# A decoder layer's 32 experts: blocks of 72 to 124 slots in float32r products in place of 64 + 32 and 128

## The chip, the core and the metric

The kernel runs on one core of one Trainium2 chip. A time is the device time of one execution, in microseconds (us); a verdict comes from the medians of repeated runs of both kernels on the same chip. Before the change three runs took 2187.02, 2189.25 and 2190.99 us, median 2189.25 us. All rows below come from one further execution, recorded by the hardware profiler, which took 2188.17 us.

Names used throughout: PE is TensorE (matmuls; PEld is its weight loading), DVE is VectorE, ACT is ScalarE, POOL is GpSimd, SP is SyncE, which issues the large loads.

## What is computed

One layer of a decoder: sliding-window attention and a convolution branch, a layer norm, then a mixture of experts and a second layer norm. Only the mixture of experts matters here. 1024 tokens of width 1024 are each sent to 4 of 32 experts, so 4096 places are shared out unevenly.

```python
logits = h @ w_router + b_router
top_val, top_idx = lax.top_k(logits, TOP_K)          # TOP_K = 4 of 32
gates = softmax(top_val)
# for each expert e, over its tokens xb:
act = clamped_swiglu(xb @ w_up[e] + b_up[e])         # 1024 -> 2048 -> 1024
ys  = act @ w_down[e] + b_down[e]                    # 1024 -> 1024
y_moe[token] += gate * ys
```

An expert has 12 MB of float32 weights (w_up 1024 x 2048, w_down 1024 x 1024). All of it is read from HBM once, whatever the number of its tokens.

## The kernel before, in words

The first 640 us (attention, convolution, output projection, router) are not touched. The mixture of experts follows, from about 640 to 2130 us, then the second layer norm to the end at 2186.6 us.

**Slots.** The router ranks the experts by the number of their tokens. The program is written for ranks, not for experts: rank j has a fixed number of slots, `CAPS[j]`, from 320 for the fullest to 64 for the emptiest, and reads at run time which expert holds the rank. Tokens beyond the slots would be done in a loop behind the main part, one block of 128 at a time; with these inputs it runs zero times. The names p0 to p31 in the profile are ranks.

**Blocks.** The slots of a rank are cut into blocks that PE works on. Before the change a block is 128, 64 or 32 slots wide. A block of 128 (called *wide* here) holds its tokens as the stationary operand, 128 columns, and streams 512 columns of weights at a time. If the rank is *split*, every weight tile and every activation is written as a high and a low part in float32r (`split`, L85 to L87: ACT copies the high part, DVE subtracts it to get the low part), and a product is three float32r matmuls: high x high, high x low, low x high (L251). A block of 64 or 32 uses the unsplit float32 weights: the columns of the PE array are divided into 2 or 4 groups, each of which works on another piece of the output columns at the same time (L260). A rank is split if it has a wide block (`self.split`); it keeps its raw weights until the matmuls are done if it also has a narrow block (`self.keep`).

**Steps.** Each expert is 12 steps of 256 rows of weights (1 MB): steps 0 to 3 and 4 to 7 make the two halves of the up projection, 8 to 11 the down projection. Ranks are worked on in pairs, `PAIRS`, so that a full and an empty one share the time in which weights arrive. Within a pair the order is: first rank's steps 0 to 3, second rank's 0 to 3, first's 4 to 7, second's 4 to 7, first's 8 to 11, second's 8 to 11: 24 steps a pair, 16 pairs.

**What sets the order.** The engines' queues are in program order, and the program is written step by step:

```python
for g, (e, s) in enumerate(G):
    split_ahead(g)      # weights split up to AHEAD = 6 half-steps ahead: this step and two more
    e.mm(s, ...)        # the matmuls of the step
    if g == 200: overflow()
    load_ahead(g)       # SP: as many 512 KB weight tiles as the 24 slots W0..W23 let it
    behind(g)           # what is due after this step, sorted by kind
```

`behind` places, among other things, for each expert: the transposes of its tokens (`x_T`, L165) shortly before its first step; after steps 3 and 7 the activation (`swiglu`, L270 to L276: bias add, sigmoid, two clamps, product; on DVE but for the sigmoid); after the step that follows, and after step 8, the transposes of the activation (`act_T`, L296), which are then split or copied; after step 11 the scaling by the gate on ACT and the scattered addition into the output in HBM on POOL's DMA queue (`scatter`, L319). So in DVE's queue an activation stands behind the splits of two later steps and ahead of all others. The program also computes, at step g = 200, which blocks the loop behind would need (`overflow`, L1227 to L1256, mostly DVE); g = 200 is the ninth step of the ninth pair.

**Biases.** For a wide block a row of 512 biases is loaded on POOL's queue (`load_row`, L210) and spread over the partitions by POOL (`bias_of`, L225). For a narrow block the DMA itself spreads it, in 2 or 4 pieces (`load_bias`, L220).

**Memory.** The 24 slots of 512 KB hold raw weights, high parts and low parts alike: a split step takes 2 raw tiles and 4 more once it is split, an unsplit one only 2.

## Time and profile before

| what | value |
|---|---|
| median of three runs | 2189.25 us |
| profiled execution | 2188.17 us |
| its span, first to last instruction | 2186.6 us |
| PE busy | 2069.1 us, 95% of the span |
| DVE busy | 1377.5 us, 63% |
| ACT busy | 878.9 us, 40% |
| POOL busy | 496.8 us, 23% |
| moved by the 16 DMA engines | 506.92 MB, 232 GB/s on the mean |

Busy shares are means over stages that differ. A matmul's recorded time reaches from its start to its modelled end, and matmuls overlap: the price of one is the distance from its start to the next one's start, not its recorded time. How the pairs of experts compare is read from the windows table among the rows below, whose stretches begin with the first matmul of a pair and end with the first of the next.

### The profile page before, as it was taken

To read this page: it belongs to the slowest core of one execution; us is meant where nothing else is said; L and a number is where in the kernel's file an instruction comes from. 1 tells how busy PE (TensorE), PEld (TensorE's weight loads), DVE (VectorE), ACT (ScalarE), POOL (GpSimd) and SP (SyncE) were. 2 spreads that over 40 slices of the span, in tenths; PEclk is the share of its full clock that TensorE was granted. 3 is DMA by queue.
4 is the path that set the end of the run, shared out by engine and by line. 5 is a ranking of instruction groups with operands and counts; after the bars stand their busy time and mean duration, and the time that the engine had idled before them with its cause. 6 is when DMAs were issued, how large, how long until landed. Compare 5 with 4: busy or idle time off the path is not lost. (4 is left out here: it accounts for less than half of the span.)

```text
span 2186.6 us, 31962 instructions
## 1 busy us (share of the span) xinstructions
PE 2069.1 (95%) x10925; PEld 1370.3 (63%) x10925; DVE 1377.5 (63%) x2052; ACT 878.9 (40%) x1337; POOL 496.8 (23%) x643
## 2 busy tenths in 40 slices
PE   8999999999959999999999999989999999999990
PEld 7776788887635566576654355556676466766760
DVE  3768799665845564656964126365596569569635
ACT  3155511432323433435653123334455357356521
POOL 1000000003332222323241322122243241232204
PEclk9999999999979999999999999999999999999995
DMA  5111112142339988998998997899889898988944
GB/s 161 41 37 30 30 49 58 34 139 64 107 116 326 313 289 301 362 347 266 319 312 296 345 333 259 283 335 328 281 312 285 307 305 303 357 259 314 346 161 162
DMA packets 191096, 506.92 MB, mean 232 GB/s; under 512 B 34700, under 2 KB 70974, under 8 KB 190929
## 3 DMA queue, kind: packets, MB, share of 16 engines
q1 hardware_dynamic: 163062, 448.86, 57.9%
q0 software_dynamic: 26592, 52.21, 9.9%
q10 hardware_dynamic: 1275, 3.77, 0.4%
q8 instruction: 87, 1.43, 0.3%
q14 instruction: 80, 0.66, 0.1%
HBM read 471.26 MB, written 33.49 MB: 231 GB/s over the span
## 5 line engine op out<-in xcount | busy, mean ns | idle before, releaser
L600 DVE SCALAR_TENSOR_TENSOR c<-a,cw,c 128x1024 f32<-128x1024 f32 x120 | 154.0, 1284 | 3.3
L828 POOL DMA_DIRECT2D bu<-in_b_up_dram x2 | 1.0, 502 | 456.4 <-DVE wol L87 456.4
L139 POOL DMA_DIRECT2D slt<-tab x103 | 54.5, 530 | 26.3 <-issue 12.5
L90 PE MATMUL ga<-xh,whga 128*128 128x512 f32 x128 | 52.1, 407 | 0.0
L92 PE MATMUL ga<-xh,wlga 128*128 128x512 f32 x128 | 50.5, 395 | 0.0
L91 PE MATMUL ga<-xl,whga 128*128 128x512 f32 x128 | 50.5, 394 | 0.0
L92 PE MATMUL gb<-xh,wlgb 128*128 128x512 f32 x128 | 50.4, 394 | 0.0
L90 PE MATMUL gb<-xh,whgb 128*128 128x512 f32 x128 | 50.4, 394 | 0.0
L91 PE MATMUL gb<-xl,whgb 128*128 128x512 f32 x128 | 50.4, 394 | 0.0
L1021 POOL DMA_INDIRECT tab<-rec,dst x32 | 32.7, 1021 | 59.5 <-DMA tab<-rec,dst 58.3
L927 PE MATMUL wo<-woh,mh 128*128 128x512 f32 x128 | 37.1, 424 | 0.6 <-ACT mh L86 0.6
L87 DVE TENSOR_TENSOR p8l<-p8w,p8h 128x1024 fp32r<-128x1024 f32 x24 | 29.5, 1281 | 10.3 <-ACT p8h L86 6.3
L927 PE MATMUL wo<-woh,ml 128*128 128x512 f32 x128 | 35.9, 404 | 0.0
L87 DVE TENSOR_TENSOR p7l<-p7w,p7h 128x1024 fp32r<-128x1024 f32 x24 | 29.3, 1270 | 9.8 <-ACT p7h L86 9.7
L927 PE MATMUL wo<-wol,mh 128*128 128x512 f32 x128 | 35.0, 409 | 0.0
L441 ACT ACTIVATE gt<-ga,pcol 128x512 f32<-128x512 f32 x16 | 11.0, 690 | 59.2 <-PE ga L92 59.1
L643 DVE SCALAR_TENSOR_TENSOR sc<-s,mask 128x512 f32<-128x512 f32 (+1 forms) x32 | 19.5, 652 | 23.9 <-PE s L640 21.8
L87 DVE TENSOR_TENSOR p0l<-p0w,p0h 128x1024 fp32r<-128x1024 f32 x24 | 29.6, 1270 | 7.4 <-ACT p0h L86 7.1
L87 DVE TENSOR_TENSOR p11l<-p11w,p11h 128x1024 fp32r<-128x1024 f32 x24 | 29.8, 1295 | 4.8 <-ACT p11h L86 4.6
L87 DVE TENSOR_TENSOR p1l<-p1w,p1h 128x1024 fp32r<-128x1024 f32 x24 | 28.5, 1241 | 5.0 <-ACT p1h L86 4.8
L87 DVE TENSOR_TENSOR p15l<-p15w,p15h 128x1024 fp32r<-128x1024 f32 x24 | 27.9, 1219 | 5.6 <-issue 4.7
L87 DVE TENSOR_TENSOR p13l<-p13w,p13h 128x1024 fp32r<-128x1024 f32 x24 | 27.9, 1219 | 5.4 <-ACT p13h L86 5.2
(1240 smaller groups left out, 6381.8 us busy)
## 6 DMA issues: line engine op xcount, KB each, us to landing
p6w<-in_w_up_dram SPq DMA_DIRECT2D x16, 512.0 KB
p31w<-in_w_up_dram SPq DMA_DIRECT2D x16, 512.0 KB
p1w<-in_w_up_dram SPq DMA_DIRECT2D x16, 512.0 KB
p30w<-in_w_up_dram SPq DMA_DIRECT2D x16, 512.0 KB
p13w<-in_w_up_dram SPq DMA_DIRECT2D x16, 512.0 KB
p19w<-in_w_up_dram SPq DMA_DIRECT2D x16, 512.0 KB
p2w<-in_w_up_dram SPq DMA_DIRECT2D x16, 512.0 KB
p29w<-in_w_up_dram SPq DMA_DIRECT2D x16, 512.0 KB
```

Source lines behind the costliest of these rows:

```text
L87: nc.vector.tensor_tensor(lo, src, hi.bitcast(F32), op=ALU.subtract)
L90: nc.tensor.matmul(o, ah, bh, start=start, stop=False)
L91: nc.tensor.matmul(o, ah, bl, start=False, stop=False)
L92: nc.tensor.matmul(o, al, bh, start=False, stop=stop)
L139: nc.gpsimd.dma_start(self.m[g * w:(g + 1) * w, i, :], tab[bass.ds(row + c, w), :])
L441: nc.scalar.activation(GT[c][:, sl], t, AF.Sigmoid, bias=bin_c(14 + c))
L600: nc.vector.scalar_tensor_tensor(C[c], A[c][:, w:w + S], cw[:, c, w:w + 1], C[c], op0=ALU.mult, op1=ALU.add)
L643: nc.vector.scalar_tensor_tensor(SC[b][c0 // 2][:, g::2, :W], t[g][:, :, :W], 0.125, mk[:, None, :].to_broadcast([P, 2, W]), op0=ALU.mult, ...
L828: nc.gpsimd.dma_start(bu, b_up[:, i * S:(i + 1) * S])
L927: nc.tensor.matmul(t, ml[:, k, :], W[k][:, sl], start=n == 0, stop=n == 3 * KC - 1)
L1021: nc.gpsimd.indirect_dma_start(out=tab[:, :], out_offset=bass.IndirectOffsetOnAxis(ap=DST[b][:, k:k + 1], axis=0), in_=REC[:, b, k, :], in ...
```

## The change

`CAPS` becomes the sum of a new table, `WIDTHS`, that gives each rank its blocks. A block is packed into column groups only if it is 64 or 32 wide; any other width is one wide block with that many columns.

- Ranks 19 to 23, before 64 + 32 slots each and not split, become single wide blocks of 96, 88, 80, 76 and 72 slots, and are split. Rank 24, before 64 + 32, becomes 64.
- 20 of the 25 wide blocks of 128 become 124 to 112 wide; those of ranks 0 and 1 and the first block of rank 9 stay at 128.
- Ranks are paired anew: before, the ranks 19 to 24 stood in the pairs (13, 19), (7, 20), (21, 22), (15, 23) and (8, 24), now in (13, 19), (20, 21), (15, 22), (8, 23) and (7, 24). Rank 3 takes the third pair position after (9, 14), with 28; the pairs (0, 27) and (4, 26) change partners among ranks of 64 slots.
- What handled 128 partitions of a wide block (bias add, sigmoid, products, scaling, gather, scatter) now handles as many as the block is wide; the low parts of its tokens and activations shrink in the free dimension.

```diff
-CAPS = [320, 288, 256, 256, 256, 256, 192, 192, 192, 160, 160, 160, 160, 128, 128, 128,
-        128, 128, 128, 96, 96, 96, 96, 96, 96, 64, 64, 64, 64, 64, 64, 64]
-PAIRS = [(6, 31), (1, 30), (13, 19), (2, 29), (9, 14), (7, 20), (21, 22), (0, 28), (15, 23), (3, 27), (10, 16), (8, 24),
-         (11, 17), (4, 26), (12, 18), (5, 25)]
+WIDTHS = [(128, 128, 64), (128, 128, 32), (124, 124), (120, 120), (116, 116), (112, 112), (120, 64), (120, 64), (112, 64),
+          (128, 32), (120, 32), (120, 32), (112, 32), (120,), (112,), (112,), (112,), (112,), (112,), (96,), (88,), (80,),
+          (76,), (72,), (64,), (64,), (64,), (64,), (64,), (64,), (64,), (64,)]
+CAPS = [sum(ws) for ws in WIDTHS]
+PAIRS = [(6, 31), (1, 30), (13, 19), (2, 29), (9, 14), (3, 28), (20, 21), (0, 27), (15, 22), (4, 26), (10, 16), (8, 23),
+         (11, 17), (7, 24), (12, 18), (5, 25)]
...
+            self.ng = [P // w if w in (32, 64) else 1 for w in widths]
+            self.np = [w * g for w, g in zip(widths, self.ng)]
+            self.wide = [g == 1 for g in self.ng]
+            self.split = fast and any(self.wide)
+            self.keep = not all(self.wide)
...
         def indices(self):
-            r = slice(0, self.nb)
-            nc.vector.tensor_copy(self.gi[:, r], self.m[:, r, 0])
             for i, (w, c) in enumerate(self.blocks):
-                if w < P:
+                nc.vector.tensor_copy(self.gi[:w, i:i + 1], self.m[:w, i, 0:1])
+                if not self.wide[i]:
...
-                    if w == P and self.split:
+                    if self.wide[i] and self.split:
                         terms = [(lhs[0], hi[kk]), (lhs[0], lo[kk]), (lhs[1], hi[kk])]
                     else:
                         terms = [(lhs[0], raw[kk])]
-                    if w == P:
+                    if self.wide[i]:
                         for h in range(2):
                             for j, (a, b) in enumerate(terms):
-                                nc.tensor.matmul(self.acc[i][h], a[:, k, :], b[:, h * 512:(h + 1) * 512],
+                                nc.tensor.matmul(self.acc[i][h][:w], a[:, k, :], b[:, h * 512:(h + 1) * 512],
...
+            tt = self.t("t", f"t{v}{i}{h}", [P, n])[:np]
+            b = self.bias[(v, i, h) if self.wide[i] else (v, i)]
+            nc.vector.tensor_tensor(tt, self.acc[i][h][:np, :n], b[:np], op=ALU.add)
...
+                av = self.act[v, i].rearrange("p (g f j) -> p g j f", f=P, j=2)
+                for q in range(4):
+                    nc.tensor.transpose(t[:, q * w:(q + 1) * w], av[:w, q // 2, q % 2, :], ident[:w, :w])
...
-        for c in sorted(set(CAPS)):
-            i, n = CAPS.index(c), CAPS.count(c)
-            nc.gpsimd.memset(capr[:, i:i + n], float(c))
+        for i, c in enumerate(CAPS):
+            nc.gpsimd.memset(capr[:, i:i + 1], float(c))
```

How the change moves instructions, at three places of the pair (13, 19). First PE's queue at rank 19's first step. Ahead of this stands the last of p13's step 3; `p19w` are raw weights, `p19h` and `p19l` high and low parts, `p19xr`, `p19xh`, `p19xl` the tokens; the size is columns of the stationary operand x streamed columns. Before, one step and the first row of the next:

```order
L260 MATMUL p19u_6794<-p19w_6528,p19xr_6672 64x512 x2
L260 MATMUL p19u_6794<-p19w_6530,p19xr_6672 64x512 x2
L260 MATMUL p19u_6795<-p19w_6528,p19xr_6725 32x256 x4
L260 MATMUL p19u_6795<-p19w_6530,p19xr_6725 32x256 x4
L260 MATMUL p19u_6794<-p19w_6564,p19xr_6672 64x512 x2
```

and now the first of the step's two halves:

```order
L254 MATMUL p19u_6810<-p19h_6739,p19xh_6718 96x512
L254 MATMUL p19u_6810<-p19l_6740,p19xh_6718 96x512
L254 MATMUL p19u_6810<-p19h_6739,p19xl_6719 96x512
L254 MATMUL p19u_6811<-p19h_6739,p19xh_6718 96x512
L254 MATMUL p19u_6811<-p19l_6740,p19xh_6718 96x512
L254 MATMUL p19u_6811<-p19h_6739,p19xl_6719 96x512
```

The packed float32 matmuls on raw weights are gone; a step of rank 19 is now 12 float32r matmuls, like one of rank 13, and needs the low parts.

Second, DVE's queue between the first activations of ranks 13 and 19 (`p13act`: end of the one; `p19t`: bias add of the other; `p13l`, `p19l`: low parts of weights, two per step). Before:

```order
L276 SCALAR_TENSOR_TENSOR p13act_6779<-p13sg_6789,p13t_6787 128x256
L87 TENSOR_TENSOR p13l_6825<-p13w_6668,p13h_6824 128x1024
L87 TENSOR_TENSOR p13l_6829<-p13w_6670,p13h_6828 128x1024
L87 TENSOR_TENSOR p13l_6845<-p13w_6713,p13h_6844 128x1024
L87 TENSOR_TENSOR p13l_6849<-p13w_6715,p13h_6848 128x1024
L270 TENSOR_TENSOR p19t_6865<-p19u_6794,p19bg_6685 128x512
```

and now:

```order
L281 SCALAR_TENSOR_TENSOR p13act_6787<-p13sg_6797,p13t_6795 120x256
L90 TENSOR_TENSOR p19l_6803<-p19w_6586,p19h_6802 128x1024
L90 TENSOR_TENSOR p19l_6807<-p19w_6588,p19h_6806 128x1024
L90 TENSOR_TENSOR p19l_6833<-p19w_6590,p19h_6832 128x1024
L90 TENSOR_TENSOR p19l_6837<-p19w_6592,p19h_6836 128x1024
L90 TENSOR_TENSOR p13l_6861<-p13w_6686,p13h_6860 128x1024
L90 TENSOR_TENSOR p13l_6865<-p13w_6688,p13h_6864 128x1024
L90 TENSOR_TENSOR p13l_6885<-p13w_6714,p13h_6884 128x1024
L90 TENSOR_TENSOR p13l_6889<-p13w_6716,p13h_6888 128x1024
L275 TENSOR_TENSOR p19t_6909<-p19u_6810,p19bc_6828 96x512
```

Between two activations DVE has eight low parts to make where it had four, those of rank 19's third and fourth steps ahead of rank 13's next.

Third, POOL's queue after the scatters of the pair before (`p1ys`), where the biases of the new pair are brought (`br`: row loaded, `bc`: row spread, `bg`: spread by the DMA). Before:

```order
L319 DMA yd<-p1ys_6582,si 4608x256
...
L210 DMA p13br_6618<-bud_69 1x16x32
L225 ISA p13bc_6683<-p13br_6593 128x512
...
L220 DMA p19bg_6685<-bud_69 64x512
...
L220 DMA p19bg_6688<-bud_70 32x256
...
L225 ISA p13bc_6736<-p13br_6618 128x512
L319 DMA yd<-p30ys_6644,si 2304x512
```

and now:

```order
L331 DMA yd<-p1ys_6600,si 4608x256
...
L213 DMA p13br_6636<-bud_69 1x16x32
L228 ISA p13bc_6690<-p13br_6611 128x512
...
L213 DMA p19br_6692<-bud_69 1x16x32
L228 ISA p13bc_6734<-p13br_6636 128x512
L331 DMA yd<-p30ys_6662,si 2304x512
...
L213 DMA p19br_6737<-bud_69 1x16x32
L228 ISA p19bc_6828<-p19br_6692 128x512
```

Six spreading DMAs of rank 19 (rows that repeat, and the register instructions between, are left out above) become two rows loaded and two spread; the second row of rank 13's bias is still issued behind the scatters of rank 1.

## Rows read from the trace of the kernel before

**Rows 1.** The page's first part: PE's busy time, share of the span, instructions.
```profile
PE 2069.1 (95%) x10925; PEld 1370.3 (63%) x10925; DVE 1377.5 (63%) x2052; ACT 878.9 (40%) x1337; POOL 496.8 (23%) x643
```

**Rows 2.** Windows: stretch, length, busy times by engine, PE clock, DMA share, GB/s.
```profile
661.10:748.90 87.80, 87.11 (x394) 44.97 (x393) 49.62 (x70) 38.25 (x53) 23.06 (x33) 0.98 0.98 337
855.50:931.00 75.50, 74.66 (x480) 41.77 (x478) 48.01 (x68) 34.84 (x50) 26.10 (x36) 1.00 1.02 362
...
1023.80:1112.50 88.70, 86.64 (x524) 62.13 (x523) 81.38 (x104) 58.30 (x75) 28.50 (x38) 1.00 0.89 297
1112.50:1210.00 97.50, 97.50 (x581) 47.49 (x579) 44.08 (x69) 31.81 (x48) 30.46 (x46) 1.00 0.93 306
1210.00:1286.00 76.00, 76.00 (x632) 26.71 (x628) 18.43 (x43) 14.07 (x30) 24.64 (x35) 1.00 1.04 353
...
1402.70:1485.70 83.00, 76.96 (x484) 43.68 (x482) 53.12 (x103) 34.86 (x50) 25.18 (x35) 0.96 0.97 331
...
1578.50:1669.50 91.00, 88.18 (x525) 63.14 (x524) 81.10 (x104) 58.49 (x75) 35.97 (x38) 0.98 0.89 294
1669.50:1767.10 97.60, 97.60 (x579) 47.69 (x577) 49.41 (x72) 36.09 (x53) 29.68 (x41) 1.00 0.93 308
...
1857.00:1949.70 92.70, 92.70 (x430) 64.58 (x429) 49.53 (x72) 35.46 (x50) 24.14 (x31) 1.00 0.93 326
```

**Rows 3.** PE's timeline in the pair (13, 19): start, us to the last end, operation.
```profile
865.73 0.39 PE L251 MATMUL p13u<-p13l,p13xh 128*128 128x512 f32 x1
...
867.99 0.39 PE L251 MATMUL p13u<-p13h,p13xl 128*128 128x512 f32 x1
868.31 11.70 PE L260 MATMUL p19u<-p19w,p19xr 128*64 128x512 f32 x96
879.94 0.50 PE L251 MATMUL p13u<-p13h,p13xh 128*128 128x512 f32 x1
```

**Rows 4.** PE's timeline in the last two pairs.
```profile
2027.85 1.03 PE L165 MATMUL p5xt<-ident,p5xg 128*128 128x128 f32 x8
...
2061.05 7.09 PE L260 MATMUL p25u<-p25w,p25xr 128*64 128x512 f32 x32
```

**Rows 5.** DVE's timeline in the pair (9, 14).
```profile
1045.43 4.63 DVE L87 TENSOR_TENSOR p14l<-p14w,p14h 128x1024 fp32r<-128x1024 f32 x4 [0.41 <-ACT p14h L86]
1049.98 4.62 DVE L87 TENSOR_TENSOR p9l<-p9w,p9h 128x1024 fp32r<-128x1024 f32 x4
1054.53 0.68 DVE L270 TENSOR_TENSOR p14t<-p14u,p14bc 128x512 f32<-128x512 f32 x1
...
1059.04 2.35 DVE L87 TENSOR_TENSOR p9l<-p9w,p9h 128x1024 fp32r<-128x1024 f32 x2
...
1068.72 0.68 DVE L270 TENSOR_TENSOR p9t<-p9u,p9bc 128x512 f32<-128x512 f32 x1
```

**Rows 6.** POOL's timeline in the pair (13, 19).
```profile
873.74 0.80 POOL L225 PARTITION_BROADCAST p13bc<-p13br  x1 [2.32 <-DMA p13br<-bud]
```

**Rows 7.** DVE's timeline in the pair (13, 19).
```profile
874.57 0.69 DVE L270 TENSOR_TENSOR p13t<-p13u,p13bc 128x512 f32<-128x512 f32 x1 [4.20 <-POOL p13bc L225]
```

**Rows 8.** DVE's timeline in the pair (15, 23); the last two are overflow's first and last.
```profile
1421.45 0.69 DVE L270 TENSOR_TENSOR p15t<-p15u,p15bc 128x512 f32<-128x512 f32 x1 [4.10 <-POOL p15bc L225]
...
1434.24 0.18 DVE L1229 TENSOR_TENSOR over<-scnt_ps,capr 128x32 f32<-128x32 f32 x1
...
1440.69 0.17 DVE L1255 CAST xci<-xcol 128x2 int32<-128x2 f32 x1
```

**Rows 9.** POOL's timeline at the end: the second scatter of rank 5.
```profile
2127.34 1.57 POOL L319 DMA_INDIRECT yd<-p5ys,gi  x1 [5.58 <-DMA yd<-p5ys,gi]
```

**Rows 10.** Windows, columns as in Rows 2: 4 us in the pair (10, 16).
```profile
1648.00:1652.00 4.00, 4.00 (x24) 2.40 (x22) 4.00 (x5) 3.15 (x4) 0.00 (x0) 0.60 0.47 173
```

**Rows 11.** PE's weight loads by form: count, busy us, mean ns, idle before.
```profile
L251 PEld LDWEIGHTS p5u<-p5h,p5xh 128*128 128x128 f32 x64 | 12.0, 188 | 3.3 <-ACT p5h L86 0.8
L260 PEld LDWEIGHTS p12u<-p12w,p12xr 128*32 128x32 f32 x128 | 3.3, 108 | 4.4 <-issue 2.8
```

More of the change, by code (lines that the diff above doesn't have):

```diff
@@ L100, with __init__ @@
     class Expert:
-        def __init__(self, pfx, cap, ev, idx, fast=True):
-            self.pfx, self.cap, self.ev = pfx, cap, ev
+        def __init__(self, pfx, widths, ev, idx, fast=True):
+            self.pfx, self.ev = pfx, ev
             self.m, self.gi, self.si = idx
-            full, rest = divmod(cap, P)
-            self.blocks = [(P, i * P) for i in range(full)]
-            c = full * P
-            for w in (64, 32):
-                if rest & w:
-                    self.blocks.append((w, c))
-                    c += w
-            self.nb = len(self.blocks)
-            self.split = fast and full > 0
-            self.keep = any(w < P for w, c in self.blocks)
+            self.blocks, c = [], 0
+            for w in widths:
+                self.blocks.append((w, c))
+                c += w
+            self.nb = len(self.blocks)
+            self.ng = [P // w if w in (32, 64) else 1 for w in widths]
[3 more added lines that the diff above has]
+            self.keep = not all(self.wide)
             self.raw, self.held, self.hi, self.lo, self.bias = {}, {}, {}, {}, {}
@@ L156, in x_T @@
             w = self.blocks[i][0]
-            if w == P and self.split:
-                self.x[i] = tuple(self.t(f"x{a}{w}", f"x{a}{i}", [P, KC, w], F32R) for a in "hl")
-            else:
-                self.x[i] = (self.t(f"xh{w}", f"xr{i}", [P, KC, w]),)
-            n = 4 if w == P else 8
+            tw = P if self.wide[i] else w
+            if self.wide[i] and self.split:
+                self.x[i] = tuple(self.t(f"x{a}{tw}", f"x{a}{i}", [P, KC, w], F32R) for a in "hl")
+            else:
+                self.x[i] = (self.t(f"xh{tw}", f"xr{i}", [P, KC, w]),)
+            n = 4 if self.wide[i] else 8
             for k0 in range(0, KC, n):
@@ L207, in load_row @@
         def load_row(self, u):
-            if any(w == P for w, c in self.blocks):
+            if any(self.wide):
                 row = self.brow[u] = self.t("brow", f"br{u}", [1, 512], bufs=BROW)
@@ L213, in load_bias @@
             for i, (w, c) in enumerate(self.blocks):
-                if w < P:
+                if not self.wide[i]:
                     ng = P // w
@@ L232, in mm @@
             if s < 8 and s % 4 == 0 or s == 8:
-                self.acc = [[acc(f"{self.pfx}{'d' if s == 8 else 'u'}{s}{i}{h}") for h in range(2 if w == P else 1)]
+                self.acc = [[acc(f"{self.pfx}{'d' if s == 8 else 'u'}{s}{i}{h}") for h in range(1 + self.wide[i])]
                             for i, (w, c) in enumerate(self.blocks)]
@@ L239, in mm @@
                 lhs = self.x[i] if s < 8 else self.aT[i]
-                ng = P // w
+                ng = self.ng[i]
                 for kk in range(2):
@@ L243, in mm @@
                     st, sp = k == 0, k == KC - 1
-                    if w == P and self.split:
+                    if self.wide[i] and self.split:
                         terms = [(lhs[0], hi[kk]), (lhs[0], lo[kk]), (lhs[1], hi[kk])]
@@ L275, in swiglu @@
             nc.vector.scalar_tensor_tensor(ln, tt[:, 0::2], LIM, ln, op0=ALU.min, op1=ALU.mult)
-            nc.vector.scalar_tensor_tensor(self.act[v, i][:, h * 256:h * 256 + n // 2], sg, SIGC, ln, op0=ALU.min,
+            nc.vector.scalar_tensor_tensor(self.act[v, i][:np, h * 256:h * 256 + n // 2], sg, SIGC, ln, op0=ALU.min,
                                            op1=ALU.mult)
         def swiglus(self, v):
-            for i, (w, c) in enumerate(self.blocks):
-                for h in range(2 if w == P else 1):
+            for i in range(self.nb):
+                for h in range(1 + self.wide[i]):
                     self.swiglu(v, i, h)
@@ L1101, in value @@
                 return ev[key]
-            return Expert(f"p{j}", CAPS[j], value, [t[:, j] for t in IDX])
+            return Expert(f"p{j}", WIDTHS[j], value, [t[:, j] for t in IDX])
         ex = [expert_of(j) for pair in PAIRS for j in pair]
```

61 lines of the change are left out of this document (32 added, 29 removed).

## The prediction, made before the changed kernel ran

> **What bounds the kernel now.** The page first: PE is busy 95% of the span [rows 1], so the question is where it is not PE. The windows, one per pair of experts, answer it [rows 2]. In the pairs that this change rewrites, (13, 19), (7, 20), (21, 22) and (8, 24), PE is busy without a gap or nearly so; DVE is busy for only 18 to 49 us of 76 to 98. The pair (9, 14) is of another sort: both ranks are split, DVE is busy for 81.38 of 88.70 us, and PE stands still for 2.06. That is the pair to learn from, since the change makes more of its sort. The DMA engines have the highest rate in the short pairs, 353 to 362 GB/s, and no wait of PE for a load shows there, because loads run far ahead.
>
> **The change on PE.** A float32r matmul costs 0.226 us from start to start (865.73 to 867.99, ten of them) [rows 3], so a step of one wide block, 12 matmuls, 2.72 us. Rank 19's first four steps, 64 + 32, take 868.31 to 879.94, 2.91 us each [rows 3]. A step of a 64 alone takes 7.09 / 4 = 1.77 us [rows 4]. Over 12 steps: 32.6 us wide, 34.9 for 64 + 32, 21.2 for 64. So ranks 19 to 23 give back 2.3 us each, 11 us together, and rank 24, which loses its 32, gives back 13.7: 25 us less of PE's work, in an engine that seems to be the bound. If nothing else mattered, this would be a gain of 1%.
>
> **What it adds on DVE.** Each of the five new split ranks has 24 low parts to make, and DVE works in order. In the pair (9, 14) eight of them in a row take 1045.43 to 1054.53, 1.14 us each; an activation of one wide block takes 1054.53 to 1059.04, 4.5 us; the next four steps' splits with one low part of an activation take 1059.04 to 1068.72, 9.7 us [rows 5]. So four steps cost DVE 14.2 us. On PE they cost, where both ranks are one wide block, 4 x 2.72 + 0.4 for transposes = 11.3 us. In (9, 14) the 32 block of rank 9 hides this; in the new pairs (13, 19), (20, 21) and (15, 22) nothing does, and each group of four up-projection steps loses 2.9 us. There are four groups. The first is paid by the lead: at the first activation two steps are already split, 5.4 us of PE's work, against 4.5 + 1.1 us until the next half step is split. Three are lost, 8.7 us; in the down projection DVE has no activation and catches up. PE's own time for such a pair is 24 x 2.72 = 65.3 plus 4.7 of transposes and changes of form (8 transposes take 1.03 us [rows 4], and some 32 occur), 70.0; as a check, (9, 14) less its 2.06 of idleness and its twelve 32-blocks of 1.1 to 1.3 us is 71 to 73. With 0.7 for the low parts of activations that PE waits for at the start of the down projection, such a pair takes 79.4 us.
>
> Two of the three get more. POOL issues the load of the second bias row behind the three scatters of rank 1, and behind those of rank 0; it waits for that load and spreads the row only at 873.74 [rows 6]. DVE waits 4.2 us for it in (13, 19) [rows 7] and 4.1 in (15, 23) [rows 8]. Today that wait is covered, since rank 19 or 23 needs nothing from DVE but its activation; with a split rank behind it in the queue PE waits as long. The row is still issued behind those scatters, so I keep 4.1 us. And (15, 22) has overflow in the middle of its up projection, 1434.24 to 1440.86, 6.6 us of DVE [rows 8], which now falls on a DVE that is behind. So: (20, 21) 79.4, (13, 19) 83.5, (15, 22) 90.1.
>
> **The sum.** The other pairs keep their kinds: (3, 28) is two wide and a 64 with a 64, like (4, 26) before and after. Removed: (7, 20), (8, 24), (13, 19), (15, 23), (21, 22), which is 97.5 + 97.6 + 75.5 + 83.0 + 76.0 = 429.6 us [rows 2]. In their place:
> - the three above, 253.0;
> - (8, 23), 97.6 less 2.3 = 95.3, DVE having some 10 us to spare there;
> - (7, 24), of the kind of (6, 31), whose 87.8 us contain 0.7 of idleness and 1.8 for a start at half clock (0.98 on the mean, so 4% of it at half [rows 2]): 85.3. By steps, 12 x (2.72 + 1.77) + 21.2 plus some 8 us of transposes and changes of form is 83. I take 84.5.
>
> Together 432.8: 3.2 us more.
>
> Small terms. The transposes of narrowed blocks shrink with the width: 16 per block cost about 2 us at 128 [rows 4], 20 blocks lose 3 to 12.5%; in the pairs where PE is the bound this is worth 1.5 us (bounds 0 and 4). In the four pairs like (9, 14), bound by DVE, four low parts of about 0.6 us [rows 5] shrink by up to an eighth: 0.3 each, 1.2. At the end, rank 5's second scatter comes 5.58 us of waiting for the first and 1.57 us of issue behind it, 7.2 us [rows 9]; with 112 rows in place of 128 that is 0.9 less (0 to 1.8). Memsets, more casts and fewer bias DMAs are on queues that wait anyway: nothing. Sum: 3.2 - 1.5 - 1.2 - 0.9 = -0.4 us on an execution of 2188.17, which stood 1.1 below the median. **Forecast: no change, 2189 us.** A difference within 0.2%, 4.4 us, is about what a measurement of this kernel can't tell from none.
>
> What the width does to a float32r matmul itself no row shows, for every one in the trace has 128 columns. The loads of the stationary operand take 188 ns for 128 columns and 108 for 32 [rows 11], 0.83 ns a column, and 188 is below the 226 between matmuls: fewer columns make a hidden load shorter. So I price the width at nothing. [...]
>
> **Rivals.**
> - *DVE keeps up* (faster): the lumps are absorbed, and the three pairs take PE's own 70, 70 and 76.6 us, 36 less: 2153. Against it: DVE's busy 81.38 of 88.70 us in (9, 14). Chance 0.10.
> - *Fewer columns make the matmul shorter* (faster): a streamed matmul costs 0.222 us in the packed 64s (7.09 / 32 [rows 4]) against 0.226. With that price, or up to 0.219, in the 12 narrowed blocks of pairs bound by PE, 144 matmuls each: 7 to 12 us, 2179. Chance 0.16.
> - *The granted clock falls* (slower): short stalls of PE before 1648 took the clock to 0.60 in a 4 us window [rows 10], half speed for most of it. The new pairs have three stalls of 2 to 4 us each. If two per pair cost 2.3 us each (91.0 of the pair around those stalls over 88.7 of (9, 14) [rows 2]), that is 14 us: 2203. It decides if PE, not DVE, is late when it runs at half speed; while DVE is late the loss is absorbed. Chance 0.18.
> - *Loads become the bound* (slower): split steps hold 6 or 4 of the 24 slots more, so loads run less far ahead. If the new pairs get their 25.2 MB at the 297 GB/s of (9, 14) [rows 2], they take 84.8: 5.4 + 1.3 more, 2196. Chance 0.10.
> - [...] Chance 0.01. The same for a rank whose tokens exceed its slots, one more block in the loop behind (12 MB loaded alone at 337 GB/s, 37 us at least): the inputs' counts all fit, the closest with one slot free. Chance 0.01.
>
> **Chances.** The forecast's own case has 0.44, 2184 to 2194: 0.31 within 0.2%, 0.08 faster, 0.05 slower. Faster: 0.08 + 0.10 + 0.16 = 0.34. Slower: 0.05 + 0.18 + 0.10 + 0.02 = 0.35. The range 2174 to 2204 leaves out DVE keeping up and the two last, 0.12, and a little of the clock's.
>
> **What would show it.** Right: windows of (13, 19), (20, 21), (15, 22) of 83, 79 and 90 us with DVE busy over 90% in their up projections and PE waiting for `l` tiles of L90; (8, 23) and (7, 24) at 95 and 84.5; matmuls 0.226 us apart at every width. Wrong: those three pairs near 70 us, or their idle time ending on DMA, or matmuls of another price by width.

## The result, and the profile after

On the same chip the changed kernel took 2227.74 us (median of 4 runs, 2221.93 to 2230.38), the kernel before 2188.34: a ratio of 1.0177, with a 95% interval of 1.016 to 1.0195. It is 39 us slower. The forecast was 2189 us, no change, in a range of 2174 to 2204: wrong, and outside the range. The profiled execution has a span of 2228.8 us, 42.2 more than before.

The page's first part after, to set beside [rows 1]:

```profile
PE 2061.4 (92%) x9973; PEld 1394.4 (63%) x9973; DVE 1525.0 (68%) x2188; ACT 987.7 (44%) x1441; POOL 497.7 (22%) x598
```

DVE is busy for 148 us more, as the change asks of it, and PE for 8 us less, but the span grows. Where, the windows per pair show (columns as in [rows 2]); these are (13, 19), (9, 14), (20, 21), (15, 22), (10, 16), (8, 23) and (7, 24):

```profile
857.90:949.90 92.00, 77.93 (x330) 55.98 (x329) 79.49 (x96) 56.30 (x70) 35.49 (x32) 0.93 0.92 277
...
1043.70:1145.00 101.30, 88.66 (x525) 61.49 (x524) 82.34 (x105) 58.56 (x76) 27.62 (x32) 0.95 0.82 258
...
1237.80:1323.00 85.20, 77.59 (x338) 50.07 (x337) 78.98 (x99) 56.93 (x72) 36.68 (x35) 0.94 0.93 307
...
1439.50:1536.70 97.20, 79.31 (x334) 54.06 (x333) 84.08 (x131) 56.78 (x71) 43.44 (x32) 0.89 0.86 265
...
1630.40:1730.50 100.10, 88.86 (x524) 60.69 (x523) 81.22 (x103) 58.14 (x75) 31.42 (x35) 0.93 0.83 265
1730.50:1826.10 95.60, 95.60 (x430) 54.56 (x429) 79.06 (x101) 57.80 (x75) 27.03 (x36) 1.00 0.91 300
...
1914.40:1997.70 83.30, 83.30 (x377) 41.49 (x376) 43.97 (x63) 33.06 (x47) 21.92 (x29) 1.00 1.01 336
```

| pair | forecast | after | over |
|---|---|---|---|
| (9, 14) | 88.7, as before | 101.3 | 12.6 |
| (10, 16) | 91.0, as before | 100.1 | 9.1 |
| (13, 19) | 83.5 | 92.0 | 8.5 |
| (20, 21) | 79.4 | 85.2 | 5.8 |
| (15, 22) | 90.1 | 97.2 | 7.1 |
| (8, 23) | 95.3 | 95.6 | 0.3 |
| (7, 24) | 84.5 | 83.3 | -1.2 |

Two separate things: 21.7 us in two pairs whose experts, pairing and order were not changed at all, only the widths of their blocks and of the ranks ahead, and 21.4 us in the three new pairs of two single wide blocks (W pairs from here on). Outside of them the differences nearly cancel: 2.5 us more lie ahead of the first pair, 5.6 us less at the very end (last section).

The first thing is a single stall per pair. These head PE's list of waits from 1030 us on (us in all, times, longest):

```profile
PE p14u L254 <- ACT p14h L89: 10.8, 1, 10.8
PE p16u L254 <- ACT p16h L89: 9.9, 1, 9.9
PE p22u L254 <- ACT p22h L89: 6.0, 1, 6.0
PE p15u L254 <- DVE p15l L90: 5.4, 1, 5.4
...
PE p20d L254 <- ACT p20ah L89: 3.4, 1, 3.4
```

ACT, which PE waits for, was itself waiting. The timeline of (9, 14) shows PE, DVE and ACT at that place:

```profile
1065.86 0.40 PE L254 MATMUL p14u<-p14h,p14xl 128*112 128x512 f32 x1
...
1072.36 0.69 DVE L275 TENSOR_TENSOR p9t<-p9u,p9bc 128x512 f32<-128x512 f32 x1 [11.47 <-POOL p9bc L228]
...
1073.09 0.43 ACT L277 ACTIVATE p9sg<-p9t 128x256 f32<-128x256 f32 x1 [13.04 <-DVE p9t L275]
...
1077.08 0.77 PE L254 MATMUL p14u<-p14h,p14xh 128*112 128x512 f32 x1 [10.82 <-ACT p14h L89]
```

DVE waits 11.47 us for the second bias row of rank 9, `p9bc`; ACT waits for DVE with a sigmoid; the high part `p14h` stands behind that sigmoid in ACT's queue, and PE behind the high part. POOL's timeline tells why the row is late. After:

```profile
1032.86 2.30 POOL L331 DMA_INDIRECT yd<-p2ys,gi  x1 [16.34 <-ACT p2ys L327]
1048.74 4.13 POOL L331 DMA_INDIRECT yd<-p2ys,gi  x1 [13.58 <-ACT p9h L89]
1051.99 1.47 POOL L213 DMA_DIRECT2D p9br<-bud  x1
...
1071.54 0.79 POOL L228 PARTITION_BROADCAST p9bc<-p9br  x1 [16.54 <-DMA p9br<-bud]
```

Before:

```profile
1012.96 1.69 POOL L319 DMA_INDIRECT yd<-p2ys,gi  x1 [15.88 <-ACT p2ys L315]
1022.59 1.79 POOL L319 DMA_INDIRECT yd<-p2ys,gi  x1 [7.94 <-ACT p9h L86]
1023.81 1.14 POOL L210 DMA_DIRECT2D p9br<-bud  x1
...
1029.93 0.91 POOL L225 PARTITION_BROADCAST p9bc<-p9br  x1 [3.25 <-DMA p9br<-bud]
```

Rank 2's second scatter is issued 15.9 us after its first (before the change: 9.6), the 2 KB of the row are asked for behind it and arrive 19.5 us later, where before they took 6. The second scatter waits for the first to land, whatever the profile names as releaser: its issue follows the end of the first one's last packet by 1.3 us after the change and 1.1 before, and in [rows 9] the wait is put down to the DMA itself. The DMA view of the stretch 1039 to 1046, in which only the first scatter runs, and, for the kernel before, of 1026 to 1028, in which its second does, show packets, MB and share of the 16 DMA engines. After:

```profile
q0 software_dynamic: 86, 0.35, 26.3%
```

Before:

```profile
q0 software_dynamic: 94, 0.39, 101.2%
```

By these shares a scatter of 128 rows keeps all 16 DMA engines busy (101.2%) and one of 124 rows about four (26.3%). From the first packet to the last, rank 2's two scatters of 124 rows take 11.2 and 13.2 us and rank 4's two of 116 rows 9.0 and 13.8; the five of 128 rows in this trace take 3.7 to 4.7, and those of 120 and 112 rows, wherever no other transfer's packets lie between theirs on the queue, 3.0 to 4.4.

### The profile page after: what moved, and what is told of

Same layout as the page of the kernel before. It is cut to its first block, busy times and chain, and to the rows that moved or that the text cites. A ratio compares the mean times of both kernels' runs of the same rounds, so it can differ in the third digit from the quotient of the medians.

```text
span 2228.8 us, 30311 instructions
## 1 busy us (share of the span) xinstructions
PE 2061.4 (92%) x9973; PEld 1394.4 (63%) x9973; DVE 1525.0 (68%) x2188; ACT 987.7 (44%) x1441; POOL 497.7 (22%) x598
## 5 line engine op out<-in xcount | busy, mean ns | idle before, releaser
L142 POOL DMA_DIRECT2D slt<-tab x74 | 39.9, 541 | 23.7 <-issue 17.7
L655 DVE SCALAR_TENSOR_TENSOR sc<-s,mask 128x512 f32<-128x512 f32 (+1 forms) x32 | 19.5, 652 | 24.0 <-PE s L652 21.8
L90 DVE TENSOR_TENSOR p23l<-p23w,p23h 128x1024 fp32r<-128x1024 f32 x24 | 27.9, 1218 | 6.6 <-ACT p23h L89 6.3
L1381 DVE BATCH_NORM_STATS2 fst<-fy 128x6 f32<-128x512 f32 x16 | 10.3, 667 | 30.8 <-DMA fy<-yd 30.8
L90 DVE TENSOR_TENSOR p5l<-p5w,p5h 128x1024 fp32r<-128x1024 f32 x24 | 28.4, 1230 | 4.0 <-ACT p5h L89 3.7
L90 DVE TENSOR_TENSOR p14l<-p14w,p14h 128x1024 fp32r<-128x1024 f32 x24 | 28.9, 1262 | 3.2 <-ACT p14h L89 3.0
```

The source lines that it names most:

```text
L90: nc.vector.tensor_tensor(lo, src, hi.bitcast(F32), op=ALU.subtract)
L142: nc.gpsimd.dma_start(self.m[g * w:(g + 1) * w, i, :], tab[bass.ds(row + c, w), :])
L655: nc.vector.scalar_tensor_tensor(SC[b][c0 // 2][:, g::2, :W], t[g][:, :, :W], 0.125, mk[:, None, :].to_broadcast([P, 2, W]), op0=ALU.mult, ...
```

## Experiments on the widths

**e1: other numbers of rows.** Theory A says that the number of rows decides how many DMA engines work on a scatter; theory B, that loads come bunched behind pairs bound by DVE and crowd the row out. (This edit and those like it show parts of the lines of `WIDTHS` and `PAIRS`.)

```diff
-(124, 124), (120, 120), (116, 116)
+(128, 120), (120, 120), (120, 112)
...
-(76,)
+(80,)
```

> The changed kernel with the slots of three ranks dealt out otherwise: rank 2 as 128 + 120 instead of 124 + 124, rank 4 as 120 + 112 instead of 116 + 116, rank 22 as 80 instead of 76; everything else as it is. Theory A (in the changed kernel's trace the scatters of 124 and of 116 rows move 12 packets of 4 KB a microsecond, those of 128, 120 and 112 rows 33 to 36; the small load of a bias row stands behind them in POOL's queue and lands 17 to 19 us after its issue, and PE stands still for 11.05 and 10.12 us): (9, 14) falls from 101.2 to 88 to 91 us, (10, 16) from 100.2 to 90 to 92, (13, 19) and (20, 21) stay within 1 us, the whole is 18 to 23 us faster than the changed kernel, 2205 to 2210. Theory B (behind the pairs that are bound by DVE the loads of weights come bunched and crowd the row out): nothing changes, 2224 to 2231. Theory C (every narrower float32r matmul and nothing else costs the time): nothing changes either.

2199.7 us, ratio 1.0063 (1.0046 to 1.008). Windows of (9, 14) and (10, 16):

```profile
1040.50:1128.90 88.40, 86.59 (x525) 60.42 (x524) 81.84 (x105) 58.48 (x76) 25.41 (x30) 1.00 0.90 296
...
1613.30:1701.60 88.30, 86.64 (x524) 59.16 (x523) 80.80 (x103) 57.86 (x75) 25.73 (x33) 1.00 0.91 297
```

Both stalls are gone; (13, 19) and (20, 21) are at 91.4 and 85.0. A holds, B falls, and so does C as the whole cause. The gain, 28 us by the medians and 25 by the ratios, is larger than the 23 expected: (10, 16) falls under what it took before, and 2 us lie ahead of the pairs.

**e3: the same in the kernel before.** Its slots and pairs, run by the changed program, with rank 2's two blocks cut:

```diff
-(128, 128), (128, 128), (128, 128)
+(124, 124), (128, 128), (128, 128)
```

> The kernel before with one thing of the change alone: rank 2's two blocks have 124 slots each instead of 128 (ranks 19 to 24 are 64 + 32 again, all other blocks 128, pairs as before). Theory A: the scatters of rank 2 run at 12 packets a microsecond, (9, 14) goes from 88.7 to 98 to 102 us, (2, 29) from 92.8 to about 94, and the whole is 10 to 14 us slower than the kernel before: 2198 to 2203. Theory B: (9, 14) stays at 88 to 89, the whole within 2 us of the kernel before, 2188 to 2190.

2207.05 us (2202.87 to 2210.68), ratio 1.0105 (1.0088 to 1.0121). A again, but my price was too low: (9, 14) takes 97.8 us, as expected, and the two pairs ahead of it lose as well, (13, 19) 78.8 for 75.5 and (2, 29) 95.7 for 92.8. There PE waits 1.6 us, ahead of the transposes, for rank 2's tokens, whose gather has 124 rows too. Pairs that the cut does not touch take what they took before, 97.5 us for (7, 20) and 76.0 for (21, 22), so the changed program itself costs nothing here. The slots of one rank, cut by 3%, cost 1% of the kernel.

**e11: which numbers.** 124, 116 and 76 are 4 x 31, 4 x 29 and 4 x 19; e1 with rank 4 as 118 + 114 asks whether the largest divisor or a multiple of 8 is the rule.

```diff
-(128, 120), (120, 120), (120, 112)
+(128, 120), (120, 120), (118, 114)
```

> e1 with rank 4's 232 slots dealt out as 118 + 114 instead of 120 + 112. In the traces so far scatters of 128, 120, 112, 96, 88 and 80 rows have 14 to 20 packets under way at once, those of 124, 116 and 76 rows 4 to 6. If a transfer is dealt out in equal parts to as many of the 16 DMA engines as divide its rows (124, 116 and 76 are 4 x 31, 4 x 29 and 4 x 19), 118 = 2 x 59 rows go to two of them: about 118 x 0.328 / 2 = 19 us, with 2 to 3 packets at once, the 114 = 6 x 19 behind it to six; (10, 16) takes over 100 us where e1 has 88.3, the whole 2212 to 2235. If numbers that 8 divides are fast and others use four engines, 118 rows take 10 to 11 us, and (10, 16) some 98 to 101.

One run: 2225.36 us. (10, 16) takes 106.0, PE waits 15.8 us at once, and the scatter of 118 rows takes 22.2 us. (15, 22) takes 102.6 for the 96.7 of e1, PE waiting 4.5 us for rank 4's tokens: the gather suffers too. POOL's timeline has the two scatters; the DMA view below it is of 1620 to 1624, in the first of them:

```profile
1609.37 2.97 POOL L331 DMA_INDIRECT yd<-p4ys,gi  x1 [14.89 <-ACT p4ys L327]
1637.19 1.88 POOL L331 DMA_INDIRECT yd<-p4ys,gi  x1 [24.85 <-issue]
```

```profile
q0 software_dynamic: 26, 0.11, 13.3%
```

13.3% is two of 16 (12.5%). The numbers 128, 124, 118 and their shares (101.2%, 26.3%, 13.3%) fit the largest divisor up to 16: 16, 4, 2. The greatest common divisor with 16 would give the same three, but not the rest: e1's scatter of 120 rows has a share of 93.3% from 1041 to 1043 us, and in the changed kernel rank 3's second, of 120 rows too, has 90.2% from 1242 to 1244, near 15 of 16 (93.75%) and not 8 (50%). The 114 rows that follow here are less clean: 27.2% from 1647 to 1650 us, 4.4 engines beside loads of weights, where the largest divisor gives 6 and the other rule 2. So the largest divisor is read off a handful of row counts, all in indirect scatters that add; for other transfers no run shows it. The prediction had only the number of rows.

**e4: the row ahead of the scatters.** Is it the scatter that hurts, or the row that stands behind it?

```diff
-                at(q - 3, e.load_row, 2 * v + 1)
+                at(q - (3 if n % 2 or v else 4), e.load_row, 2 * v + 1)
```

> The changed kernel with one edit: the load of the second bias row of a pair's first rank is issued one step earlier, beside that of the first row and so ahead of the scatters of the pair before. Widths and scatters stay as they are. If the row's landing behind the scatter is what PE's long stalls come from (theory A): the waits of 11.05, 10.12 and, in (13, 19), 5.95 us fall under 4 each, (9, 14) to 89 to 94, (10, 16) to 90 to 94, (13, 19) to 86 to 89, the whole 20 to 32 us faster than the changed kernel, 2196 to 2208. If the slow scatter hurts in another way (it keeps four DMA engines from the weights, or POOL from its next work), the stalls stay over 6 us and the whole is over 2215.

2200.38 us, ratio 1.0072 (1.0055 to 1.0089). The scatters are as slow as ever (the second one waits 13.17 us), but the row is spread at once:

```profile
1042.45 2.28 POOL L331 DMA_INDIRECT yd<-p2ys,gi  x1 [13.17 <-ACT p9h L89]
1043.87 1.67 POOL L228 PARTITION_BROADCAST p9bc<-p9br  x1
1045.84 0.58 POOL L213 DMA_DIRECT2D p14br<-bud  x1 [0.30 <-POOL p9bc L228]
1046.44 0.79 POOL L228 PARTITION_BROADCAST p9bc<-p9br  x1
```

(9, 14) takes 91.2 us, (10, 16) 89.1, (13, 19) 87.2 and (15, 22) 92.0. So the row is what nearly all of the loss goes through, all but 2.5 us in (9, 14), and in two W pairs it costs 4.8 and 5.2 us by itself.

**e2: 128 slots everywhere.**

```diff
-(124, 124), (120, 120), (116, 116), (112, 112), (120, 64), (120, 64), (112, 64),
-(128, 32), (120, 32), (120, 32), (112, 32), (120,), (112,), (112,), (112,), (112,), (112,), (96,), (88,), (80,),
-(76,), (72,)
+(128, 128), (128, 128), (128, 128), (128, 128), (128, 64), (128, 64), (128, 64),
+(128, 32), (128, 32), (128, 32), (128, 32), (128,), (128,), (128,), (128,), (128,), (128,), (128,), (128,), (128,),
+(128,), (128,)
```

> The changed kernel with all wide blocks at 128 slots, ranks 19 to 23 among them; experts split and paired as in the changed kernel. Theory A: as in e1 the two long stalls go, and float32r matmuls come every 227 ns instead of 231 to 232, so that (2, 29), (4, 26) and (5, 25) lose some 1 us each; the three pairs of two single blocks stay long, (13, 19) 89 to 92, (20, 21) 82 to 85, (15, 22) 93 to 97. Whole: 2196 to 2206. Theory B: 2220 to 2229. If the narrow width were all that costs, and DVE in the new pairs nothing: 2160 to 2180.

2199.42 us, ratio 1.0066 (1.0049 to 1.0083): what e1 has. (2, 29) takes 92.6 for 93.8 us after, (5, 25) 91.0 for 92.1. The matmuls show it: in the changed kernel's (9, 14) ten of 112 columns start from 1063.78 to 1065.86 us, 0.231 apart, where those of 128 columns stand 0.226 apart [rows 3]; the first of the ten, the last being shown above:

```profile
1063.78 0.39 PE L254 MATMUL p14u<-p14h,p14xl 128*112 128x512 f32 x1
```

The W pairs stay long, 89.2, 85.1 and 97.6. So the widths as such move little, and the W pairs are a matter of their own.

## Experiments on the pairs

**e5: row and overflow out of the W pairs.** e2 with e4's edit and

```diff
-            if g == 200:
+            if g == 176:
                 overflow()
```

> All wide blocks at 128 slots as in e2, the second bias row issued one step earlier as in e4, and the overflow computation moved 24 steps up, from the pair (15, 22) into the pair (0, 27), where DVE is busy for 53 of 116 us. If the late row and the overflow are terms of their own on top of DVE's lateness: (13, 19) falls from 89.2 to 84 to 86 us, (15, 22) from 97.6 to 84 to 88, (20, 21) stays at 85, the whole goes from 2199.4 to 2180 to 2187. If DVE's backlog absorbs them (it would be as late without them): (15, 22) stays over 92, the whole over 2190. The 5 us by which even the pair without them, (20, 21), is over the 79.4 that was forecast remain in both cases.

2184.7 us, ratio 0.9998 (0.9989 to 1.0008). Windows of the three W pairs:

```profile
853.20:938.40 85.20, 76.03 (x331) 60.27 (x330) 79.38 (x96) 57.67 (x72) 36.97 (x31) 0.96 0.94 318
...
1211.80:1299.30 87.50, 78.16 (x338) 61.68 (x337) 80.90 (x98) 58.12 (x73) 38.04 (x35) 0.94 0.92 296
...
1416.40:1501.60 85.20, 76.05 (x330) 60.21 (x329) 79.36 (x96) 57.62 (x72) 36.17 (x30) 0.96 0.93 314
```

Row and overflow are terms of their own, priced about right: (15, 22) falls by 12.4 us, for 4.1 + 6.6 in the forecast. What stays is a base of 85 to 87 us, where I had 79.4.

**e7: the control.** The kernel before's slots and pairs, and the two edits:

```diff
-                at(q - 3, e.load_row, 2 * v + 1)
+                at(q - (3 if n % 2 or v else 4), e.load_row, 2 * v + 1)
...
-            if g == 200:
+            if g == 176:
```

> The kernel before's experts, widths and pairs, with the two edits of e5 that are no part of the change: second bias row one step earlier, overflow 24 steps up. There a pair of two split ranks with two blocks does not exist; (15, 23) waits 6.0 us for overflow (as in e3's trace) and (10, 16) some 2 us for a row. Expected: (15, 23) 83.0 to 77, the whole 6 to 9 us faster than the kernel before, 2176 to 2181 on this chip. This says how much of what e5 and e6 win is the change's own: if e5 is not faster than this, splitting ranks 19 to 23 in these pairs gives nothing.

2179.52 us, ratio 0.9976 (0.9967 to 0.9986), 5 us faster than the kernel before, for 6 to 9 expected; (15, 23) falls from 83.0 to 75.4. e5 is 5 us slower than this: splitting ranks 19 to 23, in these pairs and with everything else repaired, does not pay. The sixteen pairs alone cost 11 us more (1471.8 for 1460.4 by the windows); the very end of the program gives 5.6 of them back (last section).

**e9: filling the waits.** Behind waits in a W pair the granted clock is at half for a while: in the changed kernel's (20, 21) it is 0.50 from 1273.0 to 1275.5 us and, behind the wait of 3.36 us that ends at 1299.96, from 1300.0 to 1306.5. The means of 0.96 and 0.94 above are by that 7 to 10 us at half per pair. The fillers, matmuls whose result nothing reads, stand ahead of steps 2, 6 and 10; the table `FILL` has their numbers.

```diff
...
+            if (self.pfx, s) in FILL:
+                a = self.x[0][0] if s < 8 else self.aT[0][0]
+                t = trp(f"{self.pfx}fill{s}")
+                for j in range(FILL[self.pfx, s]):
+                    nc.tensor.matmul(t, a[:, 0, :], a[:, 0:4, :].rearrange("p k t -> p (k t)"), start=True, stop=True)
```

> e5 with 4 to 14 matmuls of no use (operands that are long ready, a PSUM tile that nothing reads) ahead of the steps 2, 6 and 10 at which PE waits for a high part in the three pairs of two single blocks: 0.9 to 3.2 us of them, about as long as the waits in e5's trace, 1.0 to 3.9 us. PE then works where it stood still, and the later work waits for the same high and low parts as before. Theory A (what a wait costs these pairs is the wait and then the granted clock: 3.4 or 6.8 us at half speed behind each of six waits in e5, 23.8 us in all, so up to 12 us of PE's work): the half-speed stretches go, the three pairs fall by 2 to 4 us each, the whole from 2184.7 to 2173 to 2180. Theory B (while DVE is late, PE's half speed costs nothing, since DVE's next part would be late anyway): the stretches go, the pairs stay within 1 us, the whole at 2182 to 2187.

2184.88 us, ratio 0.9999 (0.9989 to 1.0008): theory B by the whole. The three W pairs:

```profile
855.30:942.00 86.70, 80.24 (x355) 63.81 (x354) 79.27 (x96) 57.65 (x71) 36.54 (x31) 0.98 0.95 324
...
1215.50:1299.70 84.20, 80.14 (x362) 64.01 (x361) 80.55 (x98) 57.97 (x72) 37.95 (x35) 0.98 0.93 302
...
1416.80:1503.10 86.30, 80.49 (x355) 64.96 (x354) 79.32 (x96) 57.72 (x72) 38.55 (x31) 0.96 0.93 313
```

(20, 21) falls from 87.5 to 84.2 us, its clock rising from 0.94 to 0.98; (13, 19) rises by 1.5 with a clock that rises too, (15, 22) by 1.1 with a clock that stays. Such steps in one pair say little: (20, 21) takes 84.0 to 87.5 us in the traces of e1, e2, e4, e5 and e6, where none of these edits aims at it. The half-speed stretches did not all go, as both theories had it: by the means they shrink from some 24 to some 14 us in the three pairs. That this gains nothing in the sum speaks for DVE as the bound without showing it.

**e13, e14: low parts on POOL.** Eight of a W pair's 48 low parts moved to POOL, in e5 and in e6 (below).

```diff
...
-                split(hi, lo, self.raw[s][h])
+                split(hi, lo, self.raw[s][h], nc.gpsimd if h and s in POOLS.get(self.pfx, ()) else nc.vector)
```

> e5 with 8 of the 48 low parts of weights in each of the three pairs of two single blocks made by POOL instead of DVE (second half of steps 4 to 7 of both ranks); ACT, PE and the loads as they are. In e5's trace DVE is busy for 79.4 to 80.9 of 85.2 to 87.5 us in these pairs, a low part takes it 1.15 us from start to start. Theory D (DVE's work as a whole sets the length of these pairs): DVE has 9 us less to do in each, the pairs fall by 4 to 9 us to 77 to 82, the waits at steps 6 and 10 shrink, the whole from 2184.7 to 2160 to 2173. Theory E (the lumps of 4.5 us of activation and the half-speed clock behind them set it, not DVE's sum): the pairs stay over 83, the whole over 2180. If POOL is too slow for it (an operation of this size takes it 2.3 to 3.3 us in the last part of the kernel, and its queue stands behind scatters), PE waits for low parts made on POOL and the pairs get longer than 87.

> e6 with the same 8 low parts on POOL in its one pair of that sort, (20, 21), 84.0 us in e6. Theory D: (20, 21) at 76 to 80, the whole 2163 to 2168. Theory E: as e6, 2168 to 2173. POOL too slow: 2173 or more.

2373.38 us (ratio 1.0863, 1.0845 to 1.0881) and 2227.77 us (1.0186, 1.0169 to 1.0203). Neither theory is tested: POOL was too slow, and not by the operation itself. POOL's timeline in (20, 21) of e14:

```profile
1249.26 0.80 POOL L229 PARTITION_BROADCAST p20bc<-p20br  x1 [7.58 <-issue]
...
1261.14 2.33 POOL L91 TENSOR_TENSOR p20l<-p20w,p20h 128x1024 fp32r<-128x1024 f32 x1 [7.34 <-issue]
1271.18 0.80 POOL L229 PARTITION_BROADCAST p20bc<-p20br  x1 [7.71 <-issue]
...
1280.17 6.99 POOL L91 TENSOR_TENSOR p21l<-p21w,p21h 128x1024 fp32r<-128x1024 f32 x3 [7.18 <-issue]
1296.40 0.80 POOL L229 PARTITION_BROADCAST p21bc<-p21br  x1 [9.24 <-issue]
```

Each change between spreading a row and subtracting costs POOL 7.2 to 9.2 us here, and PE waited up to 18.8 us for a low part.

**e15: low parts left out.** The same eight, in e5, are not made at all; the matmuls read the high part instead, so that this kernel leaves out a part of the products.

```diff
...
+                if h and s in NOLOW.get(self.pfx, ()):
+                    lo = hi
+                    nc.scalar.activation(hi, self.raw[s][h], AF.Copy)
+                else:
...
```

> e5, leaving out 8 of the 48 low parts of weights in each of the three pairs of two single blocks (second half of steps 4 to 7 of both ranks); the matmuls that read them read the high part in their place, so PE, ACT and the loads do what they did in e5 and DVE has some 9 us less to do per pair. This part of the products is then not computed as the reference has it. Theory D (DVE's work as a whole, 80 us of 85 to 87, sets the length of these pairs): they fall by 4 to 9 us each, to 77 to 82, the waits at steps 6 and 10 shrink, the whole from 2184.7 to 2160 to 2173. Theory E (the lumps of 4.5 us of activation and the half-speed clock behind the waits set it): the pairs stay over 83, the whole over 2180.

2168.93 us, ratio 0.9926 (0.9909 to 0.9942):

```profile
853.50:935.40 81.90, 75.11 (x331) 60.36 (x330) 70.95 (x88) 57.77 (x72) 30.38 (x31) 0.96 0.97 336
...
1208.90:1287.20 78.30, 73.80 (x338) 59.94 (x337) 72.11 (x90) 57.95 (x72) 32.86 (x35) 0.98 0.95 323
...
1404.30:1483.40 79.10, 74.67 (x331) 60.25 (x330) 70.90 (x88) 57.81 (x72) 31.17 (x30) 0.96 1.00 349
```

With PE's, ACT's and the loads' work unchanged, taking 8.4 to 8.8 us from DVE shortens the pairs by 3.3, 9.2 and 6.1 us, 18.6 of 25.7 (the first is under the 4 to 9 expected, the second, from an 87.5 that is the highest of its kind, over it; the whole is where theory D has it). In (13, 19) and (15, 22) the clock stays at 0.96, so their fall is not the clock's. Nor do the eight slots of weights that come free explain it: in e5's W pairs no wait of PE, ACT or DVE ends on a load. So DVE's work as a whole is the larger part of what sets the W pairs, some 0.7 us for each of its own; 6 to 11 us come on top of it, against 6 to 7 in e5. How much of that belongs to the clock stays open.

**e6: fewer W pairs.** e5 with one W pair left.

```diff
-(6, 31), (1, 30), (13, 19), (2, 29)
+(6, 13), (1, 30), (19, 31), (2, 29)
...
-(15, 22)
+(22, 24)
...
-(7, 24)
+(7, 15)
```

> e5 with other pairs: only one pair of two single wide blocks is left, (20, 21); the four others stand in (6, 13), (7, 15), (19, 31) and (22, 24). Theory: a pair of two split ranks with two blocks in all is bound by DVE and by what PE's clock loses, 85 us for 70 us of matmuls; a wide block beside a 64 is not. (6, 13) and (7, 15) take some 95 us like (8, 23); (19, 31) and (22, 24) have 59 us of PE's work, and 71 to 74 us of loads at the 342 to 353 GB/s of the fastest pairs, of which the run-ahead hides a part: 60 to 73 each. Five pairs of e5, some 426 us, become 395 to 421: the whole 2153 to 2180, 2165 if half is hidden. If the loads decide and nothing is hidden, 2178 to 2182; if the pairing does not matter, as in e5.

2170.61 us, ratio 0.9936 (0.9919 to 0.9952): the fastest version, 9 us under e7 and 0.6% under the kernel before. Of the 9 us some 4 lie in the sixteen pairs (1456.0 for 1460.4), the others mostly at the very end (last section). (19, 31) and (22, 24):

```profile
864.20:930.30 66.10, 63.15 (x278) 38.86 (x276) 43.23 (x59) 31.20 (x42) 23.16 (x27) 0.95 1.04 373
...
1405.00:1470.00 65.00, 60.36 (x279) 36.80 (x277) 41.66 (x58) 30.22 (x40) 21.30 (x26) 1.00 1.04 362
```

The DMA engines are full there (1.04), yet 25 MB of weights that would need 68 to 70 us at these rates cost 65 to 66; the rest must have been loaded ahead. (6, 13) as first pair takes 99.8 us, 5 more than expected.

**e8, e10, e12: variants of e6.** e8 has e1's widths, e10 fillers as in e9, e12 these fillers and the first seven pairs in another order; the edits of the last two:

```diff
+FILL = {("p20", 10): 10, ("p19", 10): 8, ("p22", 10): 8, ("p20", 6): 4, ("p21", 2): 5, ("p21", 6): 4}
...
-PAIRS = [(6, 13), (1, 30), (19, 31), (2, 29), (9, 14), (3, 28), (20, 21)
+PAIRS = [(1, 30), (6, 13), (2, 29), (19, 31), (3, 28), (9, 14), (20, 21)
```

> e6 with the widths of e1 (72 to 120 slots, none of 76, 116 or 124) instead of 128. If a float32r matmul of another width than 128 costs 4 to 5 ns more (231 to 232 ns against 227 in the traces of the changed kernel and of e2): 24 blocks of 144 matmuls, 14 to 17 us, less some 4 us of shorter transposes and what DVE or loads hide: 6 to 13 us slower than e6. If the width has no price: 0 to 5 us faster than e6.

> e6 with such fillers of 4 to 10 matmuls ahead of steps 2, 6 and 10 in (20, 21) and of step 10 in (19, 31) and (22, 24). e6 has 13.6 us at half speed in these pairs and the next one. Theory A: 2 to 6 us faster than e6, 2165 to 2169. Theory B: as e6, 2169 to 2172.

> e10 with the first seven pairs in another order: (1, 30), (6, 13), (2, 29), (19, 31), (3, 28), (9, 14), (20, 21). In e6 the first pair, (6, 13), takes 99.8 us where the like pair (7, 15) takes 95.8: its DVE starts late. With a pair first in which DVE is busy for half the time, that is hidden: (6, 13) 95 to 97, the whole 2 to 5 us faster than e10. If (19, 31) suffers behind (2, 29), whose loads leave less spare than those of (1, 30), it goes from 66 to 68 to 72 and takes that back.

e8: 2175.44 us, ratio 0.9955 (0.9938 to 0.9972), 5 us over e6, a little less than the 6 expected; the intervals overlap, but the pairs bound by PE show it, (2, 29) 93.5 for 92.8, (5, 25) 92.0 for 91.1. e10: 2172.65, ratio 0.9941 (0.9925 to 0.9958), as e6. It doesn't tell the theories apart, since the half-speed stretches moved and did not shrink: the clock of (20, 21) is 0.98 in both, that of (19, 31) rises from 0.95 to 1.00, that of (2, 29) behind it falls from 1.00 to 0.97. e12: 2173.99, ratio 0.9952 (0.9934 to 0.9969), a miss: (6, 13) falls to 96.1 as expected and (19, 31) stays at 65.5, but (1, 30) as the first pair takes 113.3 us for 106.4.

## Why the prediction was wrong

**What held.** (8, 23) and (7, 24) came out at 95.6 and 83.3 for 95.3 and 84.5. The lumps of DVE were there: PE waited at steps 2, 6 and 10 of the W pairs, for high and low parts. The late second row (4.1) and the overflow (6.6) in (13, 19) and (15, 22) were priced about right, 4.8 to 5.2 by e4 and 12.4 for both by e5. "DVE keeps up", "fewer columns make the matmul shorter" and "loads become the bound" did not come about.

**The step that failed first: "The other pairs keep their kinds".** (9, 14) and (10, 16) were left alone but for 0.3 us of low parts. The sum had a scatter only at the end, by its rows ("with 112 rows in place of 128 that is 0.9 less"; from the first issue to the second it went from 7.2 to 6.8 us there), and the small pieces of the change "on queues that wait anyway" at nothing. But scatters of 124, 116 and 76 rows are not 3 to 10% cheaper but up to three times dearer (13.8 us for 116 rows, 3.7 to 4.7 for 128), since by their shares some 4 engines in place of 16 carry them (26.3% for 124 rows, 24.6% for 116 from 1626 to 1628 us, 18.4% for 76 beside loads of weights from 1547 to 1549, against 101.2%); the row of biases behind them in POOL's queue came 19.5 us after its issue, and PE stood still for 10.8 and 9.9 us. The two pairs lost 21.7 us: e1 takes this back, e3 brings it about with the slots and pairs of the kernel before, e11 makes it worse. I had used the fact that the second row is issued behind the scatters for the W pairs only; it stands in every pair whose first rank has a wide block.

**The second: "in the down projection DVE has no activation and catches up".** The working counted, group by group, what PE loses to an activation, and reached 79.4 us. It did not add up DVE's own work for the pair: 79 to 81 us busy by the windows. 79.4 would have needed DVE busy throughout, and it does not catch up in time: the last activation of (20, 21) ends when PE has been in the down projection for 8 us, and PE waits for `p20ah`, which stands behind that activation's sigmoid in ACT's queue:

```profile
1290.50 0.39 PE L254 MATMUL p20d<-p20h,p20ah 128*88 128x512 f32 x1
...
1298.08 0.42 DVE L281 SCALAR_TENSOR_TENSOR p21act<-p21sg,p21t 80x256 f32<-80x256 f32 x1
...
1299.96 0.73 PE L254 MATMUL p20d<-p20h,p20ah 128*88 128x512 f32 x1 [3.36 <-ACT p20ah L89]
```

The base is 85 us; three times 5.8 is 17.4 of the 21.4 us that the W pairs are over. On PE's side these 5.8 are not longer waits: in (20, 21) it stands still for 7.6 us, for 9.4 in the sum. It is busy for 77.6 us in place of 70.0, and half speed makes some 5 of these (a mean of 0.94 is 10 us at half), which the sum had at nothing.

**The width.** "I price the width at nothing": in the changed kernel float32r matmuls stand 0.231 us apart at 112 columns and 0.232 at 120 (22 of rank 3, 1159.90 to 1164.77 us), not 0.226. That is some 1 us in a pair of two wide blocks, and 5 us for the whole in e8 against e6; between e1 and e2 the pairs bound by DVE, some 0.5 us shorter with narrow blocks, take it back. A weight load that gets slower with fewer columns no run shows: in the changed kernel's trace one takes 188 ns at 128 columns (`p0u`), 182 at 120 (`p3u`) and 175 at 112 (`p8u`). That is the line of 0.83 ns a column that I had drawn through two points, which by themselves could not tell. Why the matmuls stand farther apart no run shows.

**The clock's rival** saw half speed behind PE's waits coming, and it came: the W pairs have means of 0.89 to 0.94. What it is worth stays open. While DVE is late, that rival said, the loss is absorbed; e9, with fewer such stretches and the same time, agrees with that, and in e15 two pairs got shorter at the same clock.
